# Second mixer of a two-layer trunk: values, part of the gates and head 0's queries and keys by block products

## The chip, the cores and the metric

The kernel runs on one core of one Trainium2 chip, as one launch. The metric is its device time in microseconds (us), taken as the median over a few runs. PE is TensorE (matrix products), DVE is VectorE, ACT is ScalarE, POOL is GpSimd, SP is SyncE, which here issues the DMAs. SBUF is the on-chip memory, PSUM the eight banks into which PE accumulates, DRAM the memory off the core. Each engine works through its own instructions in the order the program gives.

## The reference

A trunk of two layers on x of 1024 positions by 1024 features. Layer 0 mixes positions by forgetting attention, layer 1 by gated linear attention (GLA); each is followed by a SwiGLU feed-forward of 2816 hidden units; every part has an RMS norm with shift, scale and gate from a conditioning vector (ada_w). What the change touches is layer 1's mixer, with 4 heads, 128 query and key features and 256 value features a head, and a gate r of 1024 features:

```python
h = modulate(rms_norm(x, norm1_g[1]), sh1, sc1)
q, k, v, r, a_lr = jnp.split(h @ w_in, [512, 1024, 2048, 3072], axis=-1)
log_alpha = jax.nn.log_sigmoid(a_lr @ w_a2 + b_a) / 16
b = jnp.cumsum(log_alpha, axis=chunk)          # 64 positions a chunk
...
q_in, k_in = q * jnp.exp(b), k * jnp.exp(-b)
A = tril(einsum(q_in, k_in))
o_intra = einsum(A, v)
k_dec = k * jnp.exp(b_last - b)
S_n = exp(b_last) * S_{n-1} + einsum(k_dec, v)  # state of a head, 128 x 256
o = o_intra + einsum(q_in, S_{n-1})
o = rms_norm_per_head(o) * g_o * silu(r)
x = x + g1 * (o @ w_out)
```

## The kernel before

**Numbers.** Every float32 operand is split into a rounded high part and a low part (a cast on ACT, a subtraction on DVE or POOL, helper `split`, L173 to L175). `mm3` (L285) multiplies two such pairs by three matmuls, L286 to L288: high by high, high by low, low by high. Operands are tiles of 128 partitions by 512 or 1024 columns.

**Block products.** The feed-forwards already multiply 2 by 2 blocks with seven products instead of eight: the activations give B11, B12, B21, B22 and four sums T1 to T4, the weights A11, A12, A22, A21 and S1 to S4, and the products are added up in SBUF by DVE (`prod`, L1548, and `add`, L1557). `op_raw`, `op_block`, `op_sums`, `make_s4`, `op_a12` (L843 to L897) load and split the weight blocks, the sums on POOL. `Weights` with its list `loads` (L271 and L960 on) hands the tiles out in a fixed order, a few ahead (`feed.depth`).

**Queues.** SP issues all transfers in order; a transfer that waits for its slot holds back all later ones. `weave` (L130) interleaves two generators by the costs that they yield; a scheduler then fixes each engine's order. `ada1` (L483 to L507) spends a budget at marked places on the steps of the conditioning vectors (loads `ad_s`, L414; DVE products L477); `ADA_A` and `ADA_B` are its paces.

**The second mixer.** The last chunk of layer 0's feed-forward ends with `norm_mixer` (L1789): each half of 512 positions is normed by `norm_half` (L701), even features as L710, L720, odd ones as L715, L722. For the second half, the parts of features 5 to 7 are kept in `rest_of_norm` and issued behind the first values. Then, for each head of four:

- `gv_body` (L1867): the head's values, position tile by position tile, 8 × `mm3` of 256 columns into a PSUM bank `gv_b`, split into `gvt_s`. Head 0's stand ahead of everything, those of head h + 1 behind head h.
- `gate_z`, `gate_body` (L1882, L1895): the head's decay from the rank-16 projection (`a_body`, L1856), a running sum (L1904), and exponentials on ACT (L1914, L1915) with 128 columns each.
- `head_front` (L1918): k and q by `proj` (16 × 3 matmuls of 512 columns each half, `gk_b`, `gqp_b`), times the exponentials (L1944).
- `head_back` (L1948): transposes of k, products of q and k (`at_b`), the state `Sf` (L1982) split into `S_t`, outputs `go_b` with their square sums (L2026, `gss` L2027 and L2028), scaled (`on_t`, L2030), transposed (`ogt_b`) and multiplied into the gate `gs_s` (L1995). Stored to `og_d` for heads 0 to 2.
- `r_proj` (L2034): the projections of r (`gr_b`), woven into `head_back` (L2089) as other work for PE, with SiLU on ACT (L2042).

After head 3 the head outputs are loaded back and the first half of the output projection runs by itself, `run(out_chunk(0, 4, ...))` (L2114); its second half and the norm are in the next feed-forward. In this mixer gates, decay sums and values stay in SBUF.

Of the kernel before, what the change touches and what calls it, by code (L numbers as in the profile page):

```python
# [16 lines left out]
P = 128  # L17
# [36 lines left out]
def trunk(ctx, tc, x, c, ada_w, ada_b, norm1_g, norm2_g, ffn_w_in, ffn_w_out,  # L54
# [788 lines left out]
    def op_raw(l, gr, abs_, ring=0):  # L843
# [4 lines left out]
        c0 = (gr[0] * FH if gr[0] < 2 else 0) + gr[1] * 2 * P  # L848
        k0 = 0 if gr[0] < 2 else 2 * OD * (gr[0] - 2)
        w = (ffn_w_in if gr[0] < 2 else ffn_w_out)[l]  # L850
        for ab in abs_:
            r = raw_view(ring)[:, 0:n * P].rearrange("p (k m) -> p k m", k=n)
            c1 = c0 + ab[0] * P
# [56 lines left out]

    def op_first(l, gr, ab, *loads):
        for a in loads:
            op_raw(l, *a)
        return op_block(l, gr, ab)
# [25 lines left out]

    Wg = gla_w_in[0]
# [8 lines left out]
    loads += v_loads(Wg, 1024) + [(load_w16, Wg[:, 3072:3088], "aw", ws, "all")]  # L950
    for h in range(4):
        if h:
            loads += v_loads(Wg, 1024 + h * 256)
        qk_ = w_loads(Wg, 512 + h * P) + w_loads(Wg, h * P)
        r_ = w_loads(Wg, 2048 + 2 * h * P) + w_loads(Wg, 2048 + (2 * h + 1) * P)
        loads += qk_ + r_ if h else r_[:1] + qk_ + r_[1:]
# [826 lines left out]
    hs1 = []  # L1783

    norm_banks = Ring(psp, ["b3", "b4"])
    marks = {}
    rest_of_norm, norm_end = [], []

    def norm_mixer(hf, ss, tmp):  # L1789
        if not hs1:  # L1790
            hs1.extend(new_h("h1"))
        if hf:
            marks["A"] = last_of("A")
        gates = norm_half(xs, ss, hs1, 1, hf, norm_banks, tmp, rest_of_norm if hf else None)
        if hf:
            marks.update(root_ins)
            norm_end.append(last_of("A"))
        else:
            marks["G0"] = last_of("G")
        return gates  # L1800
# [7 lines left out]
    h1 = hs1  # L1808
    after_norm = marks.pop("G0")
    split_after.update(marks)  # L1810
    dump("xb0", xs)
    x_d = tc.dram_tile([8, P, S], F32, name="x_d")
    for k in range(8):
        nc.sync.dma_start(x_d[k], xs[k])


    order = ex_sl + slots["hid"] + slots["b"][4:] + slots["to"] + x_slots + slots["b"][:4]
    fr = deque(order)
    vr = Ring(big, take(5))
    aslot, wslot = take(2)  # L1820
    Tr = Ring(big, take(3))
    gsr = Ring(big, take(2))
    qr = Ring(big, take(4))
    kir = Ring(big, take(2))
    kdr = Ring(big, take(2))
    yv = Views(take(1), 2, [HALF], "gy")
    atz = Views(take(1), 2, [4, P], "atz")
    athl = Ring(big, take(1))
    s_slot, on_slot = take(2)
    ada_v = Views(take(2), 2, [HALF], "ad").v  # L1830
    ada1_queue((2, 3, 4), ada_v[0][:, 0:256], ada_v[1:3])
    ADA_A, ADA_B = 2.6, 1.0
    rm = ada_v[3]
    nc.vector.memset(rm, 1.0)
    nc.vector.memset(rm.rearrange("p (n c) -> p n c", c=P)[:, :, 0:1], 0.0)
    og_d = tc.dram_tile([8, P, S], F32, name="og_d")
    pj, atr, kvr, opr, trr = ps_rings(3, 1, 1, 2, 1)
# [4 lines left out]
    QS = 128 ** -0.5  # L1842

    w2raw = wr([64, 512], F32, "w2raw")
    nc.sync.dma_start(w2raw[0:16, :], gla_w_a2[0])
    nc.sync.dma_start(w2raw[32:48, :], gla_w_a2[0])
    w2t = big.tile([P, 2, 512], FR, tag=wslot, name="w2t")
    aT = big.tile([P, S], FR, tag=aslot, name="aT")

    def w2_split():  # L1850
        nc.gpsimd.memset(w2t.bitcast(F32), 0.0)
        nc.gpsimd.memset(aT.bitcast(F32), 0.0)
        for r0 in (0, 32):
            split(w2t[r0:r0 + 16, 0, :], w2t[r0:r0 + 16, 1, :], w2raw[r0:r0 + 16, :])

    def a_body(aw, hf, bt):  # L1856
        ps = pj([P, HALF], F32, f"aps{hf}")
        cs = hsl(hf)
        for k in range(8):
            nc.tensor.matmul(ps, aw[:, k, :], h1[k].hi[:, cs], start=k == 0, stop=False)  # L1860
            nc.tensor.matmul(ps, aw[:, k, :], h1[k].lo[:, cs], start=False, stop=k == 7)
        a = bt[1][0:16, cs]
        sum16(a, bt[0][0:16, cs], ps)
        nc.scalar.copy(aT[0:16, cs], a)
        nc.vector.tensor_sub(aT[32:48, cs], a, aT[0:16, cs].bitcast(F32))

    def gv_body(h, wv, tp, behind=None):  # L1867

        ps = pj([P, 2, 256], F32, f"gv{h}{tp}")
        for i in range(2):  # L1870
            with tc.issue_after(behind) if behind is not None and i else ExitStack():
                run(proj_tok(ps[:, i, :], wv, h1, 2 * tp + i))
        if h:
            ada1(5.1)
        v = vr([P, 2, 2, 256], FR, f"gvt{h}{tp}")
        split(v[:, 0], v[:, 1], ps)
        return v

    def gate_tiles(h):
        return Tr([P, S], F32, f"b16_{h}"), Tr([P, S], F32, f"t2_{h}")  # L1880

    def gate_z(h, halves, bt=None):  # L1882

        b16, t2 = bt or gate_tiles(h)
        hs_ = psl(h)
        for hf in halves:
            cs = hsl(hf)
            ps = pj([P, HALF], F32, f"z{h}{hf}")
            nc.tensor.matmul(ps, w2t[:, 0, hs_], aT[:, cs], start=True, stop=False)
            nc.tensor.matmul(ps, w2t[:, 1, hs_], aT[:, cs], start=False, stop=True)  # L1890
            nc.scalar.activation(t2[:, cs], ps, AF.Abs, bias=bacol(h))
            nc.vector.tensor_scalar(b16[:, cs], ps, bacol(h), 0.0, op0=ALU.add, op1=ALU.min)
        return b16, t2

    def gate_body(h, bt=None):  # L1895


        b16, t2 = bt or gate_z(h, (0, 1))
        nc.scalar.activation(t2, t2, AF.Exp, scale=-1.0)
        nc.scalar.activation(t2, t2, AF.Ln, bias=1.0)  # L1900
        nc.vector.tensor_sub(t2, b16, t2)
        for hf in range(2):
            cs = hsl(hf)
            nc.vector.tensor_tensor_scan(b16[:, cs], rm, t2[:, cs], 0.0, ALU.mult, ALU.add)  # L1904
        b3 = b16.rearrange("p (n c) -> p n c", c=P)
        cols = sm.tile([P, 4, NB], F32, tag="dec", name=f"dec{h}")
        dec, mid, nmid, last = (cols[:, i] for i in range(4))
        nc.vector.tensor_scalar(mid, b3[:, :, CH - 1], 1.0 / 16, None, op0=ALU.mult)
        nc.vector.tensor_scalar(nmid, b3[:, :, CH - 1], -1.0 / 16, None, op0=ALU.mult)
        nc.vector.tensor_scalar(last, b3[:, :, P - 1], 1.0 / 16, None, op0=ALU.mult)  # L1910
        nc.scalar.activation(dec, last, AF.Exp)
        ei = Tr([P, S], F32, f"ei{h}")
        for n in range(NB):
            nc.scalar.activation(ei[:, psl(n)], b16[:, psl(n)], AF.Exp, scale=-1.0 / 16, bias=mid[:, n:n + 1])  # L1914
            nc.scalar.activation(t2[:, psl(n)], b16[:, psl(n)], AF.Exp, scale=-1.0 / 16, bias=last[:, n:n + 1])  # L1915
        return b16, t2, ei, (dec, nmid)

    def head_front(h, b16, t2, ei, nmid):  # L1918


        wk = feed.next()
        kin = Pair(kir([P, S], FR, f"kih{h}"), kir([P, S], FR, f"kil{h}"))
        for hf in range(2):
            cs = hsl(hf)
            ps = pj([P, HALF], F32, f"gk{h}{hf}")
            run(proj(ps, wk, h1, hf))
            ada1(5.1)
            y = yv()
            nc.vector.tensor_mul(y, ps, ei[:, cs])
            nc.vector.tensor_mul(t2[:, cs], ps, t2[:, cs])  # L1930
            split(kin.hi[:, cs], kin.lo[:, cs], y)
            for n in range(4 * hf, 4 * hf + 4):
                nc.scalar.activation(ei[:, psl(n)], b16[:, psl(n)], AF.Exp, scale=1.0 / 16, bias=nmid[:, n:n + 1])
            nc.scalar.activation(b16[:, cs], b16[:, cs], AF.Exp, scale=1.0 / 16)
        wq = feed.next()
        qt = [Pair(qr([P, S], FR, f"gq{h}{i}h"), qr([P, S], FR, f"gq{h}{i}l")) for i in range(2)]
        for hf in range(2):
            cs = hsl(hf)
            ps = pj([P, HALF], F32, f"gqp{h}{hf}")
            run(proj(ps, wq, h1, hf))  # L1940
            ada1(5.1)
            for t, f in zip(qt, (ei, b16)):
# [239 lines left out]
```

## Time and profile before

| what | value |
|---|---|
| median of 3 runs | 2395.08 us (2391.55 to 2395.37) |
| span of the profiled execution | 2392.7 us |
| busy in the span: DVE, ACT, POOL | 1770.0, 1127.9, 1046.2 us |
| moved over the span | 363.43 MB, 152 GB/s |

The span is that of one execution by the hardware profiler; the runs' times hold a little more than the span. "Busy" of an engine is the time in which it has an instruction running, over the span. The profile's "idle before" is idle time of the engine just before an instruction, and what ended it. PE's matmuls are pipelined, so a row's length (0.28 or 0.39 us) is not the spacing of two matmuls. The second mixer lies from about 1290 us to 1665 us, with the first half of the output projection to about 1727 us.

### The profile page before, as it was taken

How to read it: one execution, taken by the hardware profiler on the slowest of the kernel's cores; microseconds unless marked ns; L12 is line 12 of the kernel's file. 1: busy time of each engine (PE TensorE's matmuls, PEld its weight loads, DVE VectorE, ACT ScalarE, POOL GpSimd, SP SyncE). 2: the span in 40 equal slices, each digit the busy share in tenths (PEclk: the TensorE clock that was granted, in tenths of full speed). 3: DMA queues.
4: the chain of work that ended last, by engine and by line, in shares of the span. 5: the costliest groups of instructions: out<-in, count | busy, mean ns of one | idle time of the engine just before them, and what ended most of it. 6: DMA issues, size and time to landing. Idle time of an engine off the chain costs nothing.

```text
span 2392.7 us, 35859 instructions
## 1 busy us (share of the span) xinstructions
PE 2367.3 (99%) x12344; PEld 2017.8 (84%) x12344; DVE 1770.0 (74%) x2984; ACT 1127.9 (47%) x2164; POOL 1046.2 (44%) x974
## 2 busy tenths in 40 slices
PE   8999999999999999999999999999999999999998
PEld 7888888888888888888888888898888888888888
DVE  6577787876698788876798565655687878775787
ACT  6656565664443333345325545453343334345326
POOL 1334444533446666643264221222345666643262
PEclk9999999999999999999999999999999999999999
DMA  7423333342435545457655242334424544457664
GB/s 254 151 79 112 102 119 93 121 142 78 150 113 178 176 162 168 168 203 266 223 183 161 68 119 87 100 113 132 143 99 154 183 150 154 154 186 258 227 199 147
DMA packets 336286, 363.43 MB, mean 152 GB/s; under 512 B 24860, under 2 KB 277944, under 8 KB 336104
## 3 DMA queue, kind: packets, MB, share of 16 engines
q1 hardware_dynamic: 336104, 361.15, 46.2%
q8 instruction: 97, 1.59, 0.3%
q14 instruction: 85, 0.70, 0.1%
HBM read 268.19 MB, written 92.86 MB: 151 GB/s over the span
## 4 chain that ended last, share of the span: by engine, by line
PE 89%; DVE 3%; DMA 3%; ACT 2%; issue 1%; SPq 1%; POOL 0%; DVEq 0%; POOLq 0%; ACTq 0%
PE p_b L288 16%; PE p_b L286 16%; PE p_b L287 16%; PE o_b L1211 2%; PE t_b L1197 2%; PE qk_b L286 2%; PE qk_b L287 2%; PE qk_b L288 2%; PE vps_b L288 1%; PE vps_b L286 1%; PE vps_b L287 1%; PE gr_b L286 1%; PE gr_b L287 1%; PE gr_b L288 1%; PE s_b L1165 1%; PE s_b L1166 1%
## 5 line engine op out<-in xcount | busy, mean ns | idle before, releaser
L175 DVE TENSOR_TENSOR o_s<-xv_s,o_s 128x512 fp32r<-128x512 f32 (+1 forms) x376 | 324.4, 868 | 62.8 <-ACT o_s L174 62.4
L174 ACT CAST o_s<-xv_s 128x512 fp32r<-128x512 f32 (+1 forms) x376 | 216.1, 587 | 293.9 <-PE p_b L288 242.3
L287 PE MATMUL p_b<-B,o_s 128*128 128x512 f32 x608 | 237.5, 391 | 0.0
L288 PE MATMUL p_b<-B,o_s 128*128 128x512 f32 x608 | 236.9, 390 | 0.0
L286 PE MATMUL p_b<-B,o_s 128*128 128x512 f32 x608 | 235.6, 391 | 0.0
L876 POOL TENSOR_TENSOR ex_s<-xv_s,xv_s 128x512 f32<-128x512 f32 (+1 forms) x64 | 86.8, 1357 | 288.0 <-DMA xv_s<-in_ffn_w_in_dram 118.2
L1177 POOL TENSOR_SCALAR lp_s<-lp_s,st 128x128 f32<-128x128 f32 (+7 forms) x128 | 97.5, 765 | 248.9 <-DVE st L1176 227.2
L286 PE MATMUL p_b<-T,o_s 128*128 128x512 f32 x480 | 186.7, 389 | 0.0
L287 PE MATMUL p_b<-T,o_s 128*128 128x512 f32 x480 | 186.7, 389 | 0.0
L288 PE MATMUL p_b<-T,o_s 128*128 128x512 f32 x480 | 181.2, 389 | 0.0
L288 PEld LDWEIGHTS p_b<-B,o_s 128*128 128x128 f32 x608 | 114.5, 188 | 23.8
L286 PEld LDWEIGHTS p_b<-B,o_s 128*128 128x128 f32 x608 | 114.6, 188 | 23.8
L287 PEld LDWEIGHTS p_b<-B,o_s 128*128 128x128 f32 x608 | 114.5, 188 | 23.8
L1175 ACT ACTIVATE lp_s<-lp_s,st 128x128 f32<-128x128 f32 (+7 forms) x128 | 99.3, 777 | 61.9 <-DVE st L1171 60.0
L878 POOL TENSOR_TENSOR xv_s<-ex_s,xv_s 128x512 f32<-128x512 f32 (+1 forms) x64 | 87.6, 1368 | 60.8 <-DVE o_s L175 58.2
L174 ACT CAST pt_s<-t_b 128x512 fp32r<-128x512 f32 (+1 forms) x160 | 79.8, 547 | 72.0 <-PE t_b L1197 71.4
L1559 DVE TENSOR_TENSOR ex_s<-ex_s,p_b 128x512 f32<-128x512 f32 x140 | 93.6, 680 | 25.1 <-PE p_b L288 24.9
L227 POOL TENSOR_TENSOR w_l_s<-w__s,w_h_s 128x256 fp32r<-128x256 f32 x90 | 69.3, 798 | 91.1 <-ACT w_h_s L223 51.9
L175 DVE TENSOR_TENSOR pt_s<-t_b,pt_s 128x512 fp32r<-128x512 f32 (+1 forms) x160 | 96.3, 630 | 15.7 <-ACT pt_s L174 15.2
L287 PEld LDWEIGHTS p_b<-T,o_s 128*128 128x128 f32 x480 | 90.1, 188 | 18.7
L286 PEld LDWEIGHTS p_b<-T,o_s 128*128 128x128 f32 x480 | 90.1, 188 | 18.7
L288 PEld LDWEIGHTS p_b<-T,o_s 128*128 128x128 f32 x480 | 90.1, 188 | 18.6
(1956 smaller groups left out, 7427.6 us busy)
## 6 DMA issues: line engine op xcount, KB each, us to landing
xv_s<-in_ffn_w_in_dram SPq DMA_DIRECT2D x176, 256.0 KB, 3.4
hid_B<-x SPq DMA_DIRECT2D x70, 512.0 KB, 2.9
ad_s<-in_ada_w_dram SPq DMA_DIRECT2D x384, 64.0 KB, 2.4
hid_T<-x SPq DMA_DIRECT2D x36, 512.0 KB, 2.9
xv_s<-in_ffn_w_out_dram SPq DMA_DIRECT2D x96, 192.0 KB, 5.0
ada_s<-in_ada_w_dram SPq DMA_DIRECT2D x96, 128.0 KB, 2.9
xv_s<-in_ffn_w_out_dram SPq DMA_DIRECT2D x40, 256.0 KB, 2.9
T2o<-hid_T SPq DMA_DIRECT2D x18, 512.0 KB, 8.8
```

The lines of the kernel that those rows point to most:

```text
L174: nc.scalar.copy(hi, src)
L175: nc.vector.tensor_sub(lo, src, hi.bitcast(F32))
L227: (nc.gpsimd if i < 3 else nc.vector).tensor_sub(lo[:, cs], rw[:, cs], hi[:, cs].bitcast(F32))
L286: nc.tensor.matmul(ps, ah, bh, start=start, stop=False)
L287: nc.tensor.matmul(ps, ah, bl, start=False, stop=False)
L288: nc.tensor.matmul(ps, al, bh, start=False, stop=stop)
L876: nc.gpsimd.tensor_add(s1, a21, a22)
L878: nc.gpsimd.tensor_sub(a11, s1, a11)
L1175: nc.scalar.activation(lp, lp, AF.Exp, bias=mcur, scale=-1.0, accum_out=st[:, qi, 2:3])
L1177: nc.gpsimd.tensor_scalar(lp, lp, st[:, qi, 3:4], 1.0, op0=ALU.mult, op1=ALU.mult)
L1197: nc.tensor.transpose(tp[:, i, :], lps[qi][:, psl(2 * b + jj)], ident)
L1559: nc.vector.tensor_add(d, d if src is None else dest(G, src), ps)
```

## The change

The values of all four heads, r's tiles 0 to 3 (heads 0 and 1) and head 0's k and q are computed ahead of the heads, by seven block products each instead of eight. For that the norm makes the activations as blocks: `blocks_half` and `split_half` replace `norm_half`, and the second half is normed without the delay. T1 and T2 are made next, T3 takes B12's place (B12 goes to DRAM, `b12_d`, and comes back), then T4. The values' sums C11, C12, C22, C21 are split and stored to `v_d`; each head loads its part. The gates of all heads are computed between the matmuls of T3, T4 and the r groups, their running sums go to `cum_g`; `exps(h)` loads them and makes the exponentials. r's results go to `gs_d` without SiLU, `load_gs` loads them and applies it. The woven partner of head h is now `exps`, the r projection of tile 4 + h and the k and q of head h + 1; r's tile 7 runs by itself, and head 3 is woven with the first half of the output projection. Conditioning vector 2 is worked on during the r groups, 3 and 4 during the heads.

Core of the diff, with the new functions (weight loading by `op_v`, norm, products, heads):

```diff
+    VKINDS = ("A11", "A12", "S2", "S4", "S1", "S3", "A22")
+    MGROUPS = [(-1, 2048 + 2 * h * P, 2048 + (2 * h + 1) * P) for h in range(2)] + [(-1, 512, 0)]
...
+    def op_v(kind, k):
...
+        if kind == "S2":
+            a21, a22, y = raw(k, 1), raw(4 + k, 1), raw(k, 0)
+            nc.gpsimd.tensor_add(s1, a21, a22)
+            nc.gpsimd.tensor_sub(y, s1, y)
+        elif kind == "S3":
+            a11, y = raw(k, 0), raw(k, 1)
+            nc.gpsimd.tensor_sub(y, a11, y)
...
+        t = op_tile([HALF], f"ov{kind}{k}")
+        nc.scalar.copy(t[:, 0], y)
+        (nc.gpsimd if kind in ("A12", "A22", "S1") and k % 2 else nc.vector).tensor_sub(
+            t[:, 1], y, t[:, 0].bitcast(F32))
...
-    loads += v_loads(Wg, 1024) + [(load_w16, Wg[:, 3072:3088], "aw", ws, "all")]
-    for h in range(4):
...
+    loads += mixer_loads()
+    for h in range(1, 4):
+        loads += w_loads(Wg, 2560 + (h - 1) * P) + w_loads(Wg, 512 + h * P) + w_loads(Wg, h * P)
+    loads += w_loads(Wg, 2560 + 3 * P)
...
+    def blocks_half(hf, rb, tmp):
...
+        for k in range(8):
+            y = ys1[(hf, k)] = tmp()
+            if k % 2 == 0:
+                nc.vector.scalar_tensor_tensor(y, xs[k][:, cs], acol(1, 0, k), rb, op0=ALU.mult, op1=ALU.mult)
+            else:
+                nc.vector.tensor_mul(y, xs[k][:, cs], rb)
+                nc.scalar.activation(y, y, AF.Identity, scale=acol(1, 0, k), bias=mcol(1, 0, k))
...
+    for k in range(4):
+        nc.gpsimd.tensor_sub(y11[k], y12[k], y11[k])
+        split_block(B["T1"][k], y11[k])
+        nc.vector.tensor_sub(y11[k], y22[k], y11[k])
+        split_block(B["T2"][k], y11[k], even(k, mcol(1, 0, k + 4)))
+    split_half(1)
...
+    def v_prod(nm, g=None):
+
+        t = B[nm]
+        ps = [bk8([P, HALF], F32, f"vp{nm}{i}") for i in range(4)]
+        for k in range(4):
+            w = feed.next()
+            for i in range(4):
+                mm3(ps[i], t[k][:, 0, psl(i)], t[k][:, 1, psl(i)], w.hi, w.lo, k == 0, k == 3)
+            if g is not None:
+                next(g, None)
+        return ps
...
+    def v_add(o, i, ps):
+        for t in range(4):
+            nc.vector.tensor_add(C[o][t], C[i][t], ps[t])
...
+    a_half(0)
+    c_block("U", xsl[0:2])
+    for t, ps in enumerate(v_prod("B11")):
+        nc.scalar.copy(C["U"][t], ps)
+    c_block("11", xsl[2:4])
+    v_add("11", "U", v_prod("B21"))
+    a_half(1)
+    v_add("U", "U", v_prod("T2"))
...
+    v_out("11", xsl[6:8])
...
+    v_add("12", "U", v_prod("B22"))
...
+    ps = v_prod("T1")
+    v_add("12", "12", ps)
+    v_add("22", "U", ps)
+    v_out("12", xsl[2:3])
+    g = all_gates()
+    ps = v_prod("T3", g)
+    v_add("U", "U", ps)
+    v_add("22", "22", ps)
+    v_out("22", xsl[2:3])
...
+    v_add("21", "U", v_prod("T4", g))
+    v_out("21", xsl[2:3])
...
+    for h in range(2):
...
+        for _ in products(MGROUPS[h], dsts[h], r_fin):
+            next(g, None)
+        run(g)
+        if h == 0:
+            start_ada()
+            g = exps(0)
+    ada1.flush()
...
+    run(products(MGROUPS[2], dsts[2], lambda o: front(0, o // 2, o % 2, dsts[2][o])))
...
+    def load_v(h):
+        r = []
+        for tp in range(4):
+            t = vr([P, 2, 2, 256], FR, f"gvt{h}{tp}")
+            nc.sync.dma_start(t.bitcast(F32), v_d[h, tp])
+            r.append(t)
+        return r
...
-        weave(head_back(h, kin, qt, t2, dec, vt, gs, need), 13.0, rg, 20.8)
...
+    for h in range(3):
+        weave(head_back(h, load_v(h), load_gs(h)), 13.0, chain(exps(h + 1), r_gen(4 + h), front_gen(h + 1)), 31.2)
...
+    run(r_gen(7))
+    gs3 = load_gs(3)
+    weave(head_back(3, load_v(3), gs3), 13.0, go_tail(), 36.0)
...
-    run(out_chunk(0, 4, oh, xs, 1, 2, "go", (0, 1)))
```

`products(X, d, fin)` runs the seven products of one group of two weight columns of 128, as the feed-forward's `prod` and `add` do: 4 × `mm3` of 512 columns each, the sums in SBUF by DVE. `front` multiplies k and q by the exponentials and splits them, `front_gen` does the same for heads 1 to 3 with plain projections of 8 × `mm3`, `r_gen(j)` projects r's tile j and stores it. `a_half` is the former `a_body`. `v_out` casts a sum's high part on ACT, subtracts the low part on DVE and stores both.

More of the change, by code (lines that the diff above doesn't have):

```diff
@@ L1833, in trunk, with block @@
[L1833 to L1837, printed above, removed]
+    def block(nm, sl):
+        B[nm] = [big.tile([P, 2, HALF], FR, tag=sl[k], name=f"m{nm}{k}") for k in range(4)]
+    ds = sm.tile([P, 4], F32, tag="ds", name="dsm")
+    nc.vector.tensor_sub(ds, modc[:, 1, 0, 4:8], modc[:, 1, 0, 0:4])
+    even = lambda k, col: None if k % 2 else col
@@ new lines, in trunk @@
+    block("T1", slots["hid"])
+    block("T2", slots["b"][4:8])
+    for k in range(4):
[5 more added lines that the diff above has]
+    for k in range(4):
+        nc.sync.dma_start(b12_d[k], B["B12"][k].bitcast(F32))
+    aw = feed.next()
+    feed.depth = 5
+    aT = big.tile([P, S], FR, tag=sg[1], name="aT")
@@ new lines, in products, with prod @@
+    def products(X, d, fin):
+        def prod(t):
+            ps = pin([P, HALF], F32, "gp")
+            w = feed.next()
+            for k in range(4):
+                mm3(ps, w.hi[:, k, :], w.lo[:, k, :], t[k][:, 0], t[k][:, 1], k == 0, k == 3)
+            ada1(2.56)
+            return ps
+        add = lambda o, ps, src=None: nc.vector.tensor_add(d[o], d[o if src is None else src], ps)
+        nc.scalar.copy(d[0], prod(B["B11"]))
+        p5 = prod(B["T1"])
+        yield
+        add(1, prod(B["T2"]), 0)
+        yield
+        add(0, prod(B["B21"]))
+        fin(0)
+        yield
+        add(3, prod(B["T3"]), 1)
+        add(1, p5)
+        yield
+        add(2, prod(B["T4"]), 3)
+        fin(2)
+        add(3, p5)
+        fin(3)
+        yield
+        add(1, prod(B["B22"]), 1)
+        fin(1)
+        yield
@@ L1856, in a_body @@
[L1856 to L1877, printed above, removed]
@@ L1932, in head_front @@
[L1932 to L1942, printed above, removed]
-                y = yv()
-                nc.vector.scalar_tensor_tensor(y, ps, QS, f[:, cs], op0=ALU.mult, op1=ALU.mult)
-                split(t.hi[:, cs], t.lo[:, cs], y)
@@ L2100, in trunk @@
[L2100 to L2112 removed]
+    feed.depth = 3
@@ L2115, in trunk @@
+    rest = [s_ for s_ in rest if s_ not in late_sl] + late_sl
     slots = ffn_slots(rest)
```

496 lines of the change are left out of this document (312 added, 184 removed).

## The prediction

> **What bounds the kernel now.** I read the profile page first: the busy shares, then the chain of waits, then the costliest groups.
>
> ```profile
> span 2392.7 us, 35859 instructions
> PE 2367.3 (99%) x12344; PEld 2017.8 (84%) x12344; DVE 1770.0 (74%) x2984; ACT 1127.9 (47%) x2164; POOL 1046.2 (44%) x974
> PE 89%; DVE 3%; DMA 3%; ACT 2%; issue 1%; SPq 1%; POOL 0%; DVEq 0%; POOLq 0%; ACTq 0%
> L175 DVE TENSOR_TENSOR o_s<-xv_s,o_s 128x512 fp32r<-128x512 f32 (+1 forms) x376 | 324.4, 868 | 62.8 <-ACT o_s L174 62.4
> L1559 DVE TENSOR_TENSOR ex_s<-ex_s,p_b 128x512 f32<-128x512 f32 x140 | 93.6, 680 | 25.1 <-PE p_b L288 24.9
> ```
>
> PE sets the time: 89% of the chain is its own work. So a matmul less is worth its spacing, unless something else becomes late. The last two rows are for later: a DVE subtraction with both inputs in SBUF takes 868 ns on average, one with an input in PSUM 680.
>
> Next the windows of the second mixer, as a whole and by stretch; columns are window, length, busy us and count of each engine (PE, PEld, DVE, ACT, POOL), clock, DMA share, GB/s.
>
> ```profile
> 1290.00:1665.00 375.00, 371.52 (x2230) 330.05 (x2229) 236.23 (x426) 187.52 (x397) 95.74 (x114) 1.00 0.37 110
> 1357.00:1406.00 49.00, 46.37 (x303) 41.51 (x302) 34.38 (x70) 29.91 (x68) 9.42 (x12) 1.00 0.30 86
> 1406.00:1470.00 64.00, 64.00 (x370) 56.19 (x370) 40.70 (x78) 24.71 (x57) 14.72 (x18) 1.00 0.39 113
> 1470.00:1545.00 75.00, 74.15 (x464) 66.55 (x463) 46.33 (x91) 36.41 (x79) 14.69 (x18) 1.00 0.37 106
> 1545.00:1620.00 75.00, 75.00 (x467) 67.45 (x466) 43.78 (x81) 37.98 (x84) 17.76 (x22) 1.00 0.32 99
> 675.00:705.00 30.00, 30.00 (x134) 24.86 (x133) 30.00 (x42) 16.43 (x28) 13.14 (x7) 1.00 0.35 107
> ```
>
> PE idles 3.5 us in 375 (375.00 − 371.52), 2.6 of them in head 0 (1357 to 1406). DVE is 63% busy there and POOL 26%: the mixer has slack on both, the feed-forward (last row, 675 to 705) has none on DVE and still lets PE run.
>
> **What the change takes from PE.** I need the spacing of the two matmul shapes. Rows of the PE timeline (start, length, line, tiles), and the values' own matmuls in one window:
>
> ```profile
> 1410.47 0.28 PE L286 MATMUL gv_b<-wv_0h_s,h1h 128*128 128x256 f32 x1
> ...
> 1411.07 0.28 PE L288 MATMUL gv_b<-wv_0h_s,h1l 128*128 128x256 f32 x1
> 1290.00:1600.00 310.00, 100.27 (x768) 96.56 (x768) 10.93 (x16) 9.32 (x16) 0.99 0.35 100
> ```
>
> Five steps in 0.60 us: 0.120 us for 256 columns. For 512 columns the window 675 to 705 has 134 in 30.00 us: 0.224.
>
> Values: before, 4 heads × 8 token tiles × 8 × 3 = 768 matmuls of 256 columns, 92.2 us at 0.120; they hold PE for 100.27, so up to 8.1 us are small holes between them (or tails that other matmuls cover). After, 7 products × 4 × 4 × 3 = 336 of 512 columns, 75.3 us. Gain 16.9, or 25.0 with the holes.
>
> Gates r of heads 0 and 1 (tiles 0, 1 and 2, 3) and head 0's k and q: six projections of 48 matmuls, 288, become three groups of 7 × 12 = 252. Gain 36 × 0.224 = 8.1.
>
> The rest of PE's work is the same: 32 matmuls for the rank-16 projection, 16 for the gates, the heads' own, 384 of the output projection. The 3.5 us of visible idle belong to a schedule that no longer exists, so I credit them too and charge the new one in full. Credit: 25.0 + 8.1 + 3.5 = 36.6; at least 16.9 + 8.1 = 25.0.
>
> **What it adds, in order.** Four stretches where something other than PE can be late.
>
> (1) The transition. Before, the second half's norm was held back behind the first values. Now that half is normed at once, and B12, B22, T1, T2 are made before T2's product can end. From the root of the second half's norm to T2's last operand the order built for DVE has 49 instructions: 8 norm products, 20 low parts of blocks, 6 sums for T2 and T4, 5 low parts of weights, 4 sums of products, 4 low parts of values and two small ones; 12 have an input in PSUM, 37 have both in SBUF. POOL has 18 beside them: 4 sums for T1, 4 for T3, a sum and a low part for T4, 7 for the weights and a fill. PE's order has 165 matmuls from there to T2's end (rest of B11, B21, the second half's 16, T2, parts of B22): 165 × 0.224 = 37.0 us of cover. The prices, from the timelines of DVE and POOL (same columns):
>
> ```profile
> 1284.87 0.73 DVE L720 SCALAR_TENSOR_TENSOR te_s<-x,amul,rb_b 128x512 f32<-128x512 f32 x1
> ...
> 1289.30 0.68 DVE L722 TENSOR_TENSOR te_s<-x,rb_b 128x512 f32<-128x512 f32 x1
> 1289.89 0.82 DVE L710 SCALAR_TENSOR_TENSOR h1l<-te_s,modc,h1h 128x512 fp32r<-128x512 f32 x1
> ...
> 1291.30 1.36 DVE L710 SCALAR_TENSOR_TENSOR h1l<-te_s,modc,h1h 128x512 fp32r<-128x512 f32 x1
> ```
>
> ```profile
> 1288.86 1.31 POOL L715 TENSOR_TENSOR h1l<-te_s,h1h 128x512 fp32r<-128x512 f32 x1
> 1290.82 1.30 POOL L715 TENSOR_TENSOR h1l<-te_s,h1h 128x512 fp32r<-128x512 f32 x1 [0.65 <-ACT h1h L714]
> ```
>
> Seven steps from 1284.87 to 1289.30: 0.633 us per DVE instruction when nothing blocks; 49 make 31.0. L710 shows the blocking: the one at 1291.30 ends 0.54 us after POOL's instruction (1290.82 + 1.30 = 1292.12), so it stood still meanwhile. How much that costs on average the feed-forward window shows: 42 DVE instructions should take 26.6 us and fill 30.00, so 7 POOL instructions cost DVE 3.4 us, 0.49 each; with some POOL work spanning the window's edge I use 0.53. Then DVE needs 31.0 + 18 × 0.53 = 40.5 against 37.0: a stall of 3.5. If every POOL instruction excluded every SBUF-only one, 18 × 1.30 + 37 × 0.633 = 46.8: a stall of 9.8. I take 7, between them, since the last operands also pass POOL, ACT and DVE in turn.
>
> [...]
>
> (2) The other products: T1, T3, T4, then r and k/q. DVE's order has 151 more instructions (the sums out of PSUM, low parts of values and weights, scans, the conditioning steps of vector 2): 151 × 0.633 = 95.6; POOL's 32 cost 32 × 0.53 = 17.0; 112.6 in all against 457 matmuls, 102.4 us. What frees a PSUM bank is a DVE sum, and behind it wait the next product's matmuls. Not all of the excess of 10.2 is paid, as eight banks let PE run ahead and the work of head 0 gives DVE a few matmuls more: 8, between 0 and 13 (the page's 868 − 680 = 188 ns on the some 106 SBUF-only ones is 20, so 115.6).
>
> (3) Head 0. Its state steps now stand with little else: one r half and one k half (48 matmuls) are ordered behind the sum that ends conditioning vector 2. The chain of a step, from the groups in the window of the old head 0, POOL's from the whole mixer (count, busy us, mean ns):
>
> ```profile
> L1982 DVE SCALAR_TENSOR_TENSOR Sf<-Sf,dec,kv_b 128x256 f32<-128x256 f32 x6 | 2.8, 472 | 0.4 <-PE kv_b L288 0.4
> L175 DVE TENSOR_TENSOR S_t<-Sf,S_t 128x256 fp32r<-128x256 f32 x7 | 2.9, 415 | 0.1
> L2030 DVE TENSOR_SCALAR on_t<-go_b,gss 128x256 f32<-128x256 f32 x6 | 2.7, 477 | 1.4 <-POOL gss L2028 1.4
> L1995 DVE SCALAR_TENSOR_TENSOR gs_s<-ogt_b,vec,gs_s 128x512 f32<-128x512 f32 x2 | 1.5, 742 | 0.0
> L174 ACT CAST S_t<-Sf 128x256 fp32r<-128x256 f32 x7 | 2.8, 403 | 6.9 <-DVE Sf L1982 6.3 <-DVE Sf L1980 0.6
> L2026 ACT ACTIVATE junk<-go_b 128x256 bf16<-128x256 f32 x7 | 2.6, 378 | 2.2 <-PE go_b L288 2.2
> L2028 POOL TENSOR_TENSOR gss<-gss,mhalf 128x2 f32<-128x2 f32 x16 | 12.5, 783 | 123.3 <-DVE gss L2027 123.3
> ```
>
> A step is 0.472 + 0.403 + 0.415 = 1.29 us and some 0.6 of matmuls (two groups of three at 0.28 latency): 1.9. Six steps make 11.4, with some 50 matmuls of 256 columns, 6.0, in them: 5.4 idle. Each of the two outputs adds 0.378 + 0.783 + 2 × 0.477 + 0.742 = 2.9, of which I take half as uncovered: 2.9 together. In all 8; at least the 2.6 that the old head 0 idled with filler in hand, at most 11.4 + 5.8 − 6.0 = 11.2, and 13 with a late conditioning step in DVE's queue ahead of Sf.
>
> (4) Heads 1 to 3. PE: 3 × (144 × 0.224 + 12.6) = 134.6 us, where 12.6 is my estimate of a head's own matmuls (some 100 at 0.12). DVE was busy 40.70 + 46.33 + 43.78 = 130.8 us in the same heads; the 12 value splits (10.93/16 = 0.68 each) and the scans leave, so some 115 of 134.6 remains, and POOL's blocking. Old idle there: 0.85. I take 4, between 0 and 12.
>
> (5) Edges: the first product waits for B11's splits, 2 (0 to 3); the output projection, now beside head 3 instead of alone, may find its weights queued on SP behind the stores of the head outputs, 2 (0 to 6).
>
> What costs nothing, and its cover: the round trips of values, gates, sums and B12, by the shapes some 32 MB in 370 us, 86 GB/s on top of the 110 in the window, while the page's slices reach 266; all issues stay on SP. Ahead of a head's loads stands whatever SP waits for; the waits of SP's queue in 1290 to 1665 (total us, times, longest) show the danger:
>
> ```profile
> SPq L209 <- DVE w_l_s L227: 53.7, 5, 29.7
> ```
>
> A weight load waits there up to 29.7 us for its slot, and all later loads with it. Values are loaded into slots free long before, so I charge nothing; without that cover, a head's start is late by about 10.
>
> **Sum.** 7 + 8 + 8 + 4 + 2 + 2 = 31 against 36.6: −5.6. The profiled execution's span of 2392.7 becomes 2387.1. The median of the runs is 2395.08, 2.4 more, which I keep: 2389.5.
>
> **The rivals.** (A) Everything hides. For it: the window 675 to 705 has DVE at 30.00 of 30.00 and PE loses nothing. Against it: head 0 has no filler. Then (1), (2), (4), (5) are near 0 and (3) is 6: −30.6, 2364.5.
>
> (B) Slower: DVE, held by POOL, sets the pace from T2 to the end of the r and k/q products. The 50 POOL instructions cost DVE not 0.53 but the whole of their 1.30 whenever its next one has two SBUF inputs (about 0.7 of them): 50 × 1.30 × 0.7 = 45.5 instead of 26.5, 19.0 more, all of it on PE since both stretches are already short of cover: +13.4, 2408.5. It decides from 0.53 + 5.6 / 50 = 0.64 us per POOL instruction. For it: the row at 1291.30. Against it: the 0.49 of the feed-forward. [...]
>
> (C) The change does not do what it says for the heads: a load of values or gates comes late behind SP's waits, once, about 10: +4.4, 2399.5. For it: the 29.7 us. Against it: the old kernel had that wait and PE was idle only 3.5.
>
> **How the numbers follow.** Forecast 0.42, A 0.25, B 0.20, C 0.13. By 0.2% (4.8 us, about what a measurement of this kernel tells from no change): A and half of the forecast are faster, 0.46; most of the other half and a little of C are the same, 0.18; B, most of C and the forecast's tail are slower, 0.36. Extremes of the terms: credits 36.6 with stalls of 2.6 give −34; credits 25.0 with 9.8 + 13 + 13 + 12 + 3 + 6 = 56.8 give +31.8. Range 2367 to 2413, leaving out the outer parts of A and of B; the forecast's own is 2380 to 2399.
>
> **What would show it.** PE's matmul count falls by 468. The values' window should hold 336 matmuls; DVE 95% or more busy from T2 to the last k/q product with PE waiting for DVE by 10 to 20 us; POOL busy at twice its 26% there; head 0 with 6 to 11 us of PE idle behind Sf and gss; heads 1 to 3 above 97%. Wrong, if idle before T2 is over 15 us, if a DMA ends PE's waits in the heads, or if DVE's SBUF-only mean stays under 0.75 us in the products.

## The result, and the profile after

The changed kernel takes 2437.27 us (median of 4 runs, 2436.14 to 2438.41), the one before 2393.76 beside it: a ratio of 1.0179, 95% interval 1.0165 to 1.0194. It is 43.5 us slower, where 5.6 faster was forecast, outside the range (2367 to 2413) and beyond what the terms give at their extremes (31.8 slower).

The page after, the lines that answer to those of before:

```profile
span 2436.6 us, 35364 instructions
PE 2365.3 (97%) x11876; PEld 1991.2 (82%) x11876; DVE 1860.8 (76%) x3083; ACT 1148.3 (47%) x2154; POOL 1108.8 (46%) x996
PE 84%; DVE 6%; DMA 4%; issue 2%; ACT 1%; SPq 1%; POOL 1%; DVEq 0%; POOLq 0%; ACTq 0%
```

PE has the 468 matmuls less that were forecast, and its share of the chain falls from 89 to 84%. But "PE 2365.3 busy" is hardly less than 2367.3: a row of 512 columns is 0.39 us long where the next can start after 0.227, so the first 0.16 us of a gap counts as busy, and a matmul at a slower clock counts for longer (0.63 us at 1360.32). So the idle time (span less busy, 71.3 us for 25.4) shows only a part of what PE lost. A fuller reading is the spacing. From the trace I summed, over all matmuls of a stretch, the time from one start to the next beyond what that width takes at full rate (by the usual spacing in the two traces 0.227 us for 512 columns, 0.120 for 256, 0.110 for narrower ones, and never less than nothing); I call it lost PE time:

| stretch, lost PE us | before | after |
|---|---|---|
| end of the feed-forward to T1's product (before: to head 0) | 2.0 | 26.1 |
| T1, T3, T4 | | 1.1 |
| r and k/q groups | | 17.9 |
| head 0 | 5.4 | 14.0 |
| heads 1 and 2 | 2.5, 1.7 | 8.2, 1.8 |
| head 3 and output projection | 2.0 | 13.0 |
| sum | 13.6 | 82.1 |
| length of it all | 433.2 | 477.7 |

A head's stretch begins with its first transpose of k. Length less lost time is 419.6 before and 395.6 after. PE's own work fell by 24.0 us, and 68.5 more are lost: +44.5. Outside these stretches the two agree within 1 us.

The windows of the transition, of the groups and of the four heads after (window, length, busy us and count of PE, PEld, DVE, ACT, POOL, granted clock, DMA share, GB/s):

```profile
1296.00:1376.00 80.00, 61.55 (x257) 47.88 (x257) 71.06 (x75) 34.78 (x59) 58.62 (x40) 0.87 0.50 163
1413.00:1487.00 74.00, 61.49 (x249) 48.61 (x248) 52.08 (x76) 41.99 (x65) 25.86 (x19) 0.93 0.64 204
1487.00:1548.00 61.00, 53.63 (x272) 44.74 (x271) 43.01 (x88) 22.80 (x53) 14.94 (x17) 0.94 0.63 199
1548.00:1620.00 72.00, 69.14 (x360) 58.47 (x358) 51.54 (x101) 38.50 (x81) 23.55 (x27) 0.95 0.63 206
1620.00:1681.00 61.00, 61.00 (x331) 52.23 (x330) 44.96 (x85) 21.03 (x47) 10.47 (x13) 1.00 0.62 217
1681.00:1772.00 91.00, 84.52 (x400) 70.88 (x399) 61.21 (x103) 40.24 (x77) 31.41 (x36) 0.92 0.43 142
```

In the transition DVE is busy 71.06 of 80 us with 75 instructions, 0.95 us each, and POOL 58.62 with 40. The timelines of the two in its middle (start, length, line, tiles) show why:

```profile
1331.54 1.76 DVE L949 TENSOR_TENSOR ovS_s<-xv_s,ovS_s 128x512 fp32r<-128x512 f32 x1
1333.23 1.77 DVE L1861 TENSOR_TENSOR mB<-yb_s,mB 128x512 fp32r<-128x512 f32 x1
1334.92 1.77 DVE L1861 TENSOR_TENSOR mT<-te_s,mT 128x512 fp32r<-128x512 f32 x1
```

```profile
1331.03 1.73 POOL L1917 TENSOR_TENSOR te_s<-yb_s,te_s 128x512 f32<-128x512 f32 x1
1332.72 5.11 POOL L1999 TENSOR_TENSOR yb_s<-yb_s,yb_s 128x512 f32<-128x512 f32 x3
```

The two go in step, one instruction each in 1.69 us: on DVE 0.61 became 1.69, so a POOL instruction costs DVE 1.08 us where both work back to back, twice the 0.53 I had used. It is not quite the sum of both: 0.61 and POOL's 1.30 would be 1.91.

### The profile page after: what moved, and what is told of

Read it like the earlier page. It is cut to its first block, busy times and chain, and to the rows that moved or that the text cites. A ratio compares the mean times of both kernels' runs of the same rounds, so it can differ in the third digit from the quotient of the medians.

```text
span 2436.6 us, 35364 instructions
## 1 busy us (share of the span) xinstructions
PE 2365.3 (97%) x11876; PEld 1991.2 (82%) x11876; DVE 1860.8 (76%) x3083; ACT 1148.3 (47%) x2154; POOL 1108.8 (46%) x996
## 4 chain that ended last, share of the span: by engine, by line
PE 84%; DVE 6%; DMA 4%; issue 2%; ACT 1%; SPq 1%; POOL 1%; DVEq 0%; POOLq 0%; ACTq 0%
PE p_b L288 16%; PE p_b L287 16%; PE p_b L286 16%; PE t_b L1252 2%; PE o_b L1266 2%; PE qk_b L286 2%; PE qk_b L287 2%; PE qk_b L288 2%; PE vps_b L288 1%; PE vps_b L286 1%; PE vps_b L287 1%; PE s_b L1220 1%; PE s_b L1221 1%; SPq L414 1%; PE gf_b L287 1%
## 5 line engine op out<-in xcount | busy, mean ns | idle before, releaser
L286 PEld LDWEIGHTS p_b<-B,o_s 128*128 128x128 f32 x608 | 114.5, 188 | 23.8
L892 POOL TENSOR_TENSOR xv_s<-xv_s,xv_s 128x512 f32<-128x512 f32 x43 | 59.9, 1394 | 145.2 <-issue 91.3
```

The lines of the kernel that those rows point to most:

```text
L286: nc.tensor.matmul(ps, ah, bh, start=start, stop=False)
L892: nc.gpsimd.tensor_sub(r[A12], r[A12], r[A11])
```

## The experiments

Times are medians of four runs; the kernel before ran beside each at 2392.7 to 2395.5 us. The prediction's rival B is called theory L in the expectations (exclusion of DVE and POOL); rival N there is that DVE's own count and order decide.

**1. The values' weights without POOL's sums** (the sums are left out, so the products are of unsummed blocks):

```diff
-            nc.gpsimd.tensor_add(s1, a21, a22)
-            nc.gpsimd.tensor_sub(y, s1, y)
...
-            nc.gpsimd.tensor_sub(y, a11, y)
...
-            nc.gpsimd.tensor_add(y, y, a11)
-            nc.gpsimd.tensor_sub(y, y, s1)
```

> The values' weight blocks are used without POOL's sums (20 POOL instructions fewer; the values are then products of unsummed blocks). Theory L (DVE and POOL exclude each other, about 1.05 us of DVE for each POOL instruction in the transition): DVE's own list is unchanged, but 8 of the 19 POOL instructions of the transition are gone, so about 8 us of PE's 26 us of waiting there go, and 3 to 5 behind it: 2424 to 2428 us. Rival N (DVE's own count and the chain sum, cast, low part make the transition late, POOL only shares the time): within 3 us of 2437.

2424.16 us, ratio 1.0118 (1.0101 to 1.0134). Lost in the transition 14.0 for 26.1 (12.1 less, where L had 8), elsewhere 3 us less in all: L's reading.

**2. No elementwise work of POOL in the transition** (the sums for T1, T3 and half of T4 are left out too):

```diff
-        nc.gpsimd.tensor_sub(y11[k], y12[k], y11[k])
+        nc.scalar.copy(y11[k], y12[k])
...
-        nc.gpsimd.tensor_sub(y12[k], y22[k], y12[k])
+        nc.scalar.copy(y12[k], y22[k])
...
-        split_block(B["T4"][k], y21[k], pool=k % 2 == 0)
+        split_block(B["T4"][k], y21[k])
```

> As the run without weight sums, and the sums for T1, T3 and half of T4 are ACT copies instead (the sums are left out), T4's low parts on DVE: POOL has no elementwise work in the transition. Theory L: the mean of DVE's two-input low parts in the transition falls from 1.0 to 1.6 us to about 0.69, DVE's 49 instructions take about 31 us instead of 50, PE's waiting there falls from 26 to under 10: 2409 to 2417 us. Rival N: at most 6 us less than 2437.

2417.89 us, ratio 1.0092 (1.0077 to 1.0107), 1 us above the stated span. The same instructions of DVE, in the group view of the transition (count, busy us, mean ns), first after, then here:

```profile
L1861 DVE TENSOR_TENSOR mB<-yb_s,mB 128x512 fp32r<-128x512 f32 x4 | 4.9, 1226 | 0.5 <-ACT mB L1860 0.5
L1864 DVE SCALAR_TENSOR_TENSOR mB<-yb_s,modc,mB 128x512 fp32r<-128x512 f32 x4 | 6.3, 1584 | 0.0
L1919 DVE TENSOR_TENSOR te_s<-yb_s,te_s 128x512 f32<-128x512 f32 x4 | 4.3, 1068 | 0.0
```

```profile
L1856 DVE TENSOR_TENSOR mB<-yb_s,mB 128x512 fp32r<-128x512 f32 x4 | 2.8, 688 | 0.0
L1859 DVE SCALAR_TENSOR_TENSOR mB<-yb_s,modc,mB 128x512 fp32r<-128x512 f32 x4 | 3.0, 750 | 0.0
L1914 DVE TENSOR_TENSOR te_s<-yb_s,te_s 128x512 f32<-128x512 f32 x4 | 2.8, 688 | 0.0
```

1226 becomes 688 ns, 1584 becomes 750; lost time in the transition falls to 2.8. DVE's list there is no shorter (77 instructions for 75), so N falls. The transition's stall comes from POOL's work. That it acts through DVE the trace of after supports: from 1340.2 us to the matmul at 1359.7 the chain that ended last runs almost wholly through DVE, with instructions of 1.67 us in it. These two runs also take away POOL's own time as a link ahead of T2's operands, and don't part the two.

**3. T2 first**: the splits of B12, B22 and the first value block, T3 and T4 are put behind T2's last split on each engine.

```diff
+    with behind_t2():
+        split_half(1)
...
+    with behind_t2():
+        v_out("11", xsl[6:8])
```

> Nothing is left out; the splits of B12 and B22, the splits of the finished value block, T3 and T4 are ordered behind T2's last split on DVE, ACT and POOL. If the order within the transition is what costs (T2's last operand stands 48th on DVE): T2's product starts about 12 us sooner and PE's waiting falls by 6 to 12: 2425 to 2431 us. If the total of DVE and POOL in the stretch decides, the wait only moves from T2 to B22 and T3: within 3 us of 2437.

2447.61 us, ratio 1.0213 (1.0193 to 1.0233), above both stated spans. Lost until T1's product 17.7, but 9.8 behind it (1.1 before): 27.5 for 27.2, so there the wait only moved, as the second reading had it; head 0 lost 9.8 more (23.8), which neither reading had.

**4. Plain projections for r of heads 0 and 1 and head 0's k and q**:

```diff
-        for a, n in zip(MGROUPS, MGROUPS[1:] + [None]):
+        for g in MGROUPS:
+            r += w_loads(Wg, g[1]) + w_loads(Wg, g[2])
```

> r of heads 0 and 1 and head 0's k and q by plain projections (288 matmuls) instead of block products (252); the values stay block products. PE gains 36 matmuls, 8.1 us. If the 13 us of PE's waiting between 1413 and 1480 us come from the block products' weights and sums (20 weight tiles with POOL sums, 21 sums of results), they go: 2430 to 2434 us. If they come from the scans, the conditioning steps and the loads that stand in the same queues, they stay: 2442 to 2447 us.

2429.95 us, ratio 1.0144 (1.0129 to 1.0159), at the lower end of the first span: 7 faster than after with 36 matmuls more. The window of the groups here, in the columns of before:

```profile
1416.00:1481.00 65.00, 65.00 (x288) 53.81 (x288) 34.83 (x47) 36.62 (x60) 26.86 (x25) 1.00 0.76 242
```

PE doesn't wait at all (0.1 lost for 17.9). The waits of after in its groups (us in total, times, longest), PE's first and then ACT's, name the chain:

```profile
PE gp_b L286 <- ACT o1-151211_s L174: 5.1, 1, 5.1
PE gp_b L286 <- DVE gd_s L2112: 4.9, 3, 3.6
...
ACT w_h_s L223 <- DMA w__s<-in_gla_w_in_dram: 15.2, 2, 9.5
```

A cast of the heads' first weights stood in ACT's order ahead of a weight block's and waited for its load, and PE waited 5.1 us for that block; another 4.9 us PE waited for DVE's sums to free a bank. That the loss goes with the block products this run shows; the split into these two waits is a reading of the trace. To save 36 matmuls, 8.1 us, the block products cost 17.8.

**5. A store buffer of its own for r in the heads**:

```diff
-    ada1_queue((3, 4), ada_v[0][:, 0:256], ada_v[1:4])
+    ada1_queue((3, 4), ada_v[0][:, 0:256], ada_v[1:3])
...
-            y = yv()
+            y = ada_v[3]
             nc.scalar.copy(y, ps)
             nc.sync.dma_start(gs_d[j][:, hsl(hf)], y)
```

> r's woven projections are copied to a buffer of their own before they go to DRAM, instead of the two that k and q of the next head pass through (taken from the third landing buffer of the conditioning loads, which have two then). In head 0, DVE stood 4.3 us for that store, with the state's Sf behind it. If such a wait in DVE's order is what leaves PE idle in the heads, 14.0 us of lost PE time in head 0 become 9 to 11 and the kernel takes 2432 to 2435 us. If the state chain without other PE work is the cause, or the two landing buffers make the conditioning steps wait longer, no gain: 2436 to 2441 us.

2442.57 us, ratio 1.0197 (1.0181 to 1.0212): no gain, and the heads lose 37.0 us in all as after. DVE's wait of 4.3 us for that store is gone, so it was not what left PE idle. But the edit takes a landing buffer from the conditioning loads, and DVE's longest wait for one in head 0 rose from 1.8 to 3.6 us; a small gain may be hidden.

**6. The transition's sums on DVE**, nothing left out (28 instructions move, 2 more than the expectation counts):

```diff
-        nc.gpsimd.tensor_sub(y11[k], y12[k], y11[k])
+        nc.vector.tensor_sub(y11[k], y12[k], y11[k])
...
-            nc.gpsimd.tensor_add(s1, a21, a22)
-            nc.gpsimd.tensor_sub(y, s1, y)
+            nc.vector.tensor_add(s1, a21, a22)
+            nc.vector.tensor_sub(y, s1, y)
```

> Nothing is left out: the sums for T1, T3, T4, T4's low parts and the weight sums S2 and S4 are moved from POOL to DVE, which gets 26 instructions more up to T1's product, some 18 of them in the transition. Theory L: a POOL sum costs DVE 1.05 us by exclusion, the same sum on DVE 0.61, so the transition gets shorter: DVE needs about 42 us instead of 50, PE's lost time there falls from 26 to 14 to 20: 2425 to 2431 us. Rival N (DVE's count decides): 18 x 0.61 = 11 us longer, 2444 to 2450 us.

2442.18 us, ratio 1.0197 (1.0182 to 1.0212): neither. The transition did as L said, 18.0 lost for 26.1, with more work on DVE; but the groups lost 1.7 more, head 0 8.2 more. What PE gained ahead it gave back behind, for a cause that no run here shows. Experiments 9 and 10 repeat this with the groups plain.

**7. Few conditioning steps** (14 of 16 load steps of vectors 2, 3 and 4 are left out):

```diff
-        steps, got = deque(range(32 // nt)), deque()
+        few = l == 1 and j in (2, 3, 4)
+        steps, got = deque(range(2 if few else 32 // nt)), deque()
```

> Conditioning vectors 2, 3 and 4 of layer 1 are made from 2 of their 16 load steps each (14 of 16 are left out, with their DVE instructions). If the landing waits of these steps in DVE's order, and their bursts on SP ahead of the heads' loads, cause the idle of the heads, the lost PE time of head 0, head 1 and head 3 (14.0, 8.2, 13.0 us) falls to 5 to 7, 3 and 4: 2413 to 2420 us. If the unfilled state chain is the cause, only DVE's relief of some 17 us spread over 350 counts: 2431 to 2437 us.

2428.77 us, ratio 1.0144 (1.0128 to 1.0159), between the two stated spans. The groups lose 12.9 for 17.9; the heads 32.8 for 37.0. But 6.4 of the 32.8 lie between head 0's first transpose and the last matmul of the groups, where the changed kernel itself lost 0.2: PE waits 3.4 us there for B12 to come back from DRAM, a round trip that the prediction charged nothing. Without that stretch the heads lose 26.5. So the conditioning steps are a part of the heads' loss here, 4 to 10 of 37 us, and not the whole.

**8. Faster conditioning in the heads, and more other work beside head 0.** First the pace (1.7 and 0.8 for 2.2 and 1.0):

> The conditioning steps of vectors 3 and 4 are spent faster (1.7 and 0.8 for 2.2 and 1.0), so that they end before head 3. The 5.4 us and 1.5 us gaps of head 3 behind a landing go, 13.0 lost becomes 5 to 7, heads 0 to 2 get 1 to 3 worse: 2430 to 2434 us. If the gap is the head's own chain: 2436 to 2440 us.

2444.59 us, ratio 1.0212 (1.0194 to 1.0231). This is above both spans. Head 3 loses 1.8 for 13.0, less than the 5 to 7 expected, but heads 1 and 2 lose 12.7 and 14.7 for 8.2 and 1.8: the loss moved with the steps. Then r's tiles 2 and 3 woven into head 0:

```diff
+        more = () if h else (r_gen(2), r_gen(3))
+        weave(head_back(h, load_v(h), load_gs(h)), 13.0,
+              chain(exps(h + 1), *more, r_gen(4 + h), front_gen(h + 1)), 31.2 if h else 52.0)
```

> r's tiles 2 and 3 are plain projections woven into head 0 (96 matmuls) instead of a group of block products ahead of it (84), and conditioning vector 2 is worked on in the heads. PE gets 12 matmuls more, 2.7 us. If head 0 loses PE time because its own steps have too little other PE work beside them, its lost 14.0 us become 5 to 7 and one group's share of the products' 17.9 (6 to 9) goes: 2423 to 2429 us. If a wait behind a load or a store decides there, the loss stays: 2437 to 2441 us.

2441.37 us, ratio 1.0191 (1.0176 to 1.0206), in time at the span for no gain. Yet head 0 is cured (1.8 for 14.0); heads 1 to 3 lose 5.0, 10.1 and 20.9. This run also moved vector 2's steps into the heads and changed their pace (1.8 and 0.8), so it doesn't separate the two.

**9 and 10. Plain groups and a filled head 0, with the transition's sums on DVE and on POOL**:

> The run that fills head 0, with the remaining groups (r tiles 0 and 1, head 0's k and q) as plain projections too, and all sums of the transition on DVE. PE 8.1 us more than after; lost time of the products 17.9 to about 1, transition 26 to 18, head 0 14 to 6: 2405 to 2414 us. If lost time only moves from place to place, above 2425.

> As the one before, with the transition's sums on POOL as after. Theory L: 6 to 9 us slower than that one, as DVE has slack behind the transition now and the gain there is not given back; rival N: 8 to 12 us faster than that one, as DVE has 26 instructions less.

2427.36 us (ratio 1.0141, 1.0124 to 1.0158) and 2432.61 us (1.0158, 1.0143 to 1.0174). With the sums on DVE the transition loses 18.5, with POOL 26.0, and the medians are 5.3 us apart. L had 6 to 9, N 8 to 12 the other way: 28 instructions more on DVE do not make the kernel slower, which speaks for L and against N. How much faster they make it is less sure, as the single times overlap (2425.5 to 2432.1 and 2430.4 to 2435.9). The first run misses its own range by 13 us, for the heads still lose 41.2: lost time moved, as its other reading had it.

**11. The first of these with few conditioning steps** (14 of 16 load steps of vectors 2 to 4 left out):

> The run with DVE's sums, plain projections and the filled head 0 (2427 us, 41 us of PE time lost in the heads), with conditioning vectors 2, 3 and 4 made from 2 of 16 load steps each (the others are left out). There the heads have 96 matmuls more beside their steps than after. If the heads lose time because conditioning steps that wait for a landing stand ahead of the state's instructions in DVE's order, 41 us become 12 to 18: 2398 to 2406 us. If the head's own chain through PE, DVE, ACT and POOL is the limit at this length, over 30 stay lost: 2414 to 2422 us.

2405.94 us, ratio 1.0046 (1.0030 to 1.0063), at the upper end of the first span. The heads lose 21.0 for 41.2, where 12 to 18 was expected.

**12 and 13. Conditioning in layer 0's feed-forward**, all work done, and the kernel before with the same move:

```diff
-    ADA_A, ADA_B = 6.0, 3.0
-    ffn(0, oh, xs, slots, "fo", lambda: mid(0, 1), norm_mixer)
+    ADA_A, ADA_B = 2.4, 1.2
+    ffn(0, oh, xs, slots, "fo", lambda: mid(0, 1, 2, 3, 4), norm_mixer)
```

> Nothing is left out: the kernel with DVE's sums, plain projections and the filled head 0, whose conditioning vectors 2, 3 and 4 are worked on in layer 0's feed-forward together with 0 and 1, at 2.4 and 1.2 for 6.0 and 3.0. If the heads need only be free of these steps, and the feed-forward hides 48 steps more as it hides 32: 2405 to 2411 us. If its DVE (100% in places) cannot, PE loses 10 to 20 us there: 2416 to 2428 us.

> The kernel before with the same move of the conditioning vectors, as a control. Its heads lose 11.6 us of PE time in all and have other PE work: if conditioning harms only heads with little other PE work, 2390 to 2394 us where the feed-forward hides the steps, 2400 to 2414 us where it doesn't.

2453.91 us (ratio 1.0258, 1.0236 to 1.0281) and 2441.12 us (1.0197, 1.0181 to 1.0212): both far above every stated span, as the feed-forward can't hide the steps and ends about 50 us later in both (the mixer starts at 1345.8 and 1341.9 instead of 1294.3). The heads show what the steps cost. The windows of the four heads, changed kernel with the steps elsewhere:

```profile
1505.00:1586.00 81.00, 81.00 (x421) 68.69 (x419) 36.95 (x64) 36.87 (x81) 25.86 (x30) 1.00 0.37 120
1586.00:1647.00 61.00, 61.00 (x332) 52.10 (x331) 32.19 (x59) 25.94 (x59) 16.77 (x20) 1.00 0.38 126
1647.00:1711.00 64.00, 64.00 (x338) 53.97 (x336) 35.25 (x62) 25.04 (x51) 13.43 (x16) 1.00 0.52 189
1711.00:1787.00 76.00, 72.08 (x346) 60.23 (x345) 55.76 (x92) 36.90 (x74) 30.00 (x33) 0.96 0.42 139
```

Lost there 1.8, 1.8, 2.1 and 9.5, together 15.2 for 41.2 in experiment 9. The old kernel's heads lose 8.3 instead of 11.6. So the steps cost these heads 26.0 us and those of before 3.3. That the difference is the other PE work beside them is argued from the kernels' orders; no run gives heads 1 to 3 their old work back. None of these kernels beats the one before.

## Why the prediction was wrong

**PE's own work** was right. Forecast 16.9 + 8.1 = 25.0 of matmuls, measured 24.0; forecast 8.1 + 3.5 = 11.6 of holes and old idle, measured 13.6 lost by the old schedule. In all 36.6 forecast, 37.6 measured.

**The stalls** were forecast at 31 and measured 82.1. Every large term was too small, and each passed its stated upper bound.

(1) The transition: forecast 7 (and 2 at the edge), measured 26.1. Two steps failed, the price of 0.53 us per POOL instruction and the 37.0 us of cover.

The price: I took it from a feed-forward window where 7 POOL instructions stand among 42 of DVE. From the first norm product (1312.18) to T2's last split (1361.01 + 0.69) DVE took 49.5 us, where 40.5 was forecast. It has 48 instructions there, 30.4 us at 0.633, so it was held for some 18 to 19 us; POOL has not 18 beside them but 22 and two fills. That makes 0.8 to 0.9 us each (an estimate): 1.08 where DVE's instruction has two SBUF inputs, as in the rows above, and nothing where it reads PSUM (the norm products, which read rb_b there, still follow each other in 0.60 to 0.66 beside POOL's instructions of 1.32, 1.29 and 1.29 us from 1311.84, 1313.24 and 1315.75). Rival B's mechanism, and its 0.91, fit this stretch. The exclusion is nearly whole there, 1.69 us a step where the sum of both would be 1.91. The 9.8 that the prediction worked out with every POOL instruction excluding every SBUF-only one was too small as well.

The cover: this is the larger part. In those 49.5 us only 109 matmuls ran, 24.7 us at full rate, where I had counted 165, and 49.5 − 24.7 = 24.8; PE lost 25.1 there, and its waits up to then sum to 18.3, over the 15 that I had named as a sign of being wrong. The rest of T2 and B22 stood in PE's order behind operands out of the same queues. Its longest wait, 7.25 us up to 1354.67 (shown in the last section), ended with ACT's cast of a weight block for B22. POOL's sum for that block had ended at 1352.90, and ACT's order had it behind a cast that waited for DVE's te_s:

```profile
1350.03 1.75 DVE L1864 SCALAR_TENSOR_TENSOR mT<-yb_s,dsm,mT 128x512 fp32r<-128x512 f32 x1
1351.70 1.75 DVE L1919 TENSOR_TENSOR te_s<-yb_s,te_s 128x512 f32<-128x512 f32 x1
...
1351.19 1.71 POOL L942 TENSOR_TENSOR xv_s<-xv_s,ex_s 128x512 f32<-128x512 f32 x1
```

So of the 21.3 us between 24.8 and the 3.5 that my sum gave, 9.0 are DVE's time and 12.3 the cover.

(2) The groups and products: forecast 8, measured 19.0. The step that failed is the comparison of totals of DVE and PE. By the waits, two orders decided instead, ACT's behind a late load and DVE's ahead of the banks; experiment 4 shows that the loss goes with the block products. The size of DVE's total was not the cause: DVE is busy 52.08 of 74 us there, and from T2's first matmul to head 0 (1331 to 1487) 126.07 of 156, 81% where I had named 95 as the sign.

(3) and (4) Heads: head 0 forecast 8, measured 14.0; heads 1 to 3 forecast 4, measured 10.0 for heads 1 and 2 and, with the output projection (forecast 2), 13.0 for head 3. For head 0 the mechanism was right, its own steps with little else beside them, and the size was wrong; filling it with other matmuls takes 14.0 to 1.8 (experiment 8). For heads 1 to 3 the step that failed is that the term counts DVE's instructions and none of its waits: it compares DVE's busy time with PE's, and a late conditioning step ahead of Sf stands only in head 0's upper bound. Rows of DVE in head 3 after, the wait of PE that they led to, and DVE's waits for conditioning loads over the heads and the output projection, before and after:

```profile
1682.02 0.69 DVE L175 TENSOR_TENSOR kd_s<-kdt_b,kd_s 128x512 fp32r<-128x512 f32 x1 [0.44 <-ACT kd_s L174]
1684.14 0.75 DVE L1370 SCALAR_TENSOR_TENSOR x<-go050p_b,modc,x 128x512 f32<-128x512 f32 x1 [1.44 <-PE go050p_b L288]
1689.14 0.48 DVE L477 SCALAR_TENSOR_TENSOR ad_s<-ad_s,c 128x256 f32<-128x256 f32 x1 [4.24 <-DMA ad_s<-in_ada_w_dram]
1689.54 0.42 DVE L2277 COPY Sf<-kv_b 128x256 f32<-128x256 f32 x1
...
PE kv_b L286 <- DVE Sf L2277: 6.0, 2, 5.1
...
DVE ad_s L477 <- DMA ad_s<-in_ada_w_dram: 27.4, 15, 3.6
...
DVE ad_s L477 <- DMA ad_s<-in_ada_w_dram: 13.2, 11, 4.2
```

L477 waits 4.24 us for its load, Sf behind it waits with it, and PE waits 5.1 us for Sf. Before, DVE waited longer for such loads (27.4 us, 13.2 after), and PE had the next head's values to do. So the wait isn't new, and that less covers it now is the likely cause, though no run gives heads 1 to 3 that cover back. Taking the steps away alone (7) saves 4 to 10 us, filling head 0 alone (8) moves the loss to the later heads, and in the filled kernel the heads lose 20 to 26 less without the steps (11, 12). Which of the remaining 15 to 21 us are the state's chain and which the order of the output projection stays open.

Rival A had nothing for it. Rival C, a late load of a head's data, came once and small (PE waited 2.8 us for values). B, DVE held by POOL from T2 to the end of the products, was right for the transition alone, and there it lacked the cover; the groups and the heads were lost by orders that none of the rivals had.

## What to carry to other kernels

Price an instruction by the neighbours it will have, not by an average from a stretch with a different mix: where DVE and POOL both work from SBUF back to back, count their times as nearly one queue (1.69 us for 0.61 and 1.30 here). Cover counts only as far as PE's order lets it run: matmuls whose operands come out of the same queue are no cover. Work that fills PE also hides waits elsewhere; before taking it away, list every wait it covered, also those of loads that stand in another engine's order. And sums of busy time say nothing of in-order queues: name what stands ahead of the instruction that PE needs.

## What was not expected of the hardware

PE's clock fell after its waits. PE's timeline in the transition after (start, length), and the clock of three windows:

```profile
1347.04 0.39 PE L288 MATMUL vpB_b<-ovS_s,mB 128*128 128x512 f32 x1
1354.67 1.65 PE L286 MATMUL vpB_b<-ovS_s,mB 128*128 128x512 f32 x3 [7.25 <-ACT ovS_s L948]
1359.72 0.80 PE L286 MATMUL vpB_b<-ovS_s,mB 128*128 128x512 f32 x1 [3.41 <-DVE ex_s L269]
1360.32 0.63 PE L287 MATMUL vpB_b<-ovS_s,mB 128*128 128x512 f32 x1
1360.75 0.63 PE L288 MATMUL vpB_b<-ovS_s,mB 128*128 128x512 f32 x1
1361.17 0.63 PE L286 MATMUL vpB_b<-ovS_s,mB 128*128 128x512 f32 x1
...
1363.22 0.40 PE L286 MATMUL vpT_b<-ovS_s,mT 128*128 128x512 f32 x1
1363.46 0.39 PE L287 MATMUL vpT_b<-ovS_s,mT 128*128 128x512 f32 x1
```

```profile
1345.00:1356.00 11.00, 3.75 (x14) 2.51 (x12) 11.00 (x8) 1.82 (x4) 11.00 (x7) 0.70 0.47 141
1356.00:1362.00 6.00, 2.59 (x6) 1.83 (x6) 5.94 (x8) 1.80 (x4) 3.22 (x4) 0.50 0.43 137
1362.00:1376.00 14.00, 14.00 (x61) 11.51 (x60) 12.86 (x16) 4.70 (x9) 9.47 (x8) 0.96 0.37 114
```

After the waits of 7.25 and 3.41 us the granted clock is 0.50 and 512 columns take 0.43 us; at 1363.22, 3.5 us after work began again, they take 0.24. Within the stretches of the table the trace has 64 matmuls that stand in runs of five or more at over one and a half times their spacing, worth 11.9 us of the 82.1 (before: 16, 1.5). Most of these runs stand behind a gap of 2.8 to 7.4 us. Shorter gaps stand ahead of such a run, too: PE idled 1.04, 0.33, 0.90 and 0.58 us before the nine slow matmuls from 1553.7 (0.43 us each), and the granted clock from 1553 to 1556 is 0.50. The prediction had no term for it: such a run costs 1.2 to 2.4 us on top of the wait.
